# k and q of the last MoBA heads in seven block products instead of eight

## The chip, the cores and the metric

The kernel runs on one core of a Trainium2 chip. The metric is the device time of one launch in microseconds; the kernel before takes 423.49 us, the median of three runs from 423.46 to 423.8. Five engines work side by side and each takes its instructions in order: TensorE (PE in the profile; PEld is its weight load), VectorE (DVE), ScalarE (ACT), GpSimd (POOL) and SyncE (SP), which here only issues transfers. An instruction that waits holds up all that stand behind it on its engine or queue.

## The reference, cut to what matters

The input x has 512 tokens of 1024 values. One normalised copy h is multiplied by a wide matrix; its columns give q, k, v and z of eight forgetting heads and of eight MoBA heads, two gates, and the forget logits. Head dimension is 64, so half of the heads are 256 columns.

```python
h = rms_norm(x, norm_g)
proj = h @ w_in
fq, fk, fv, fz, mq, mk, mv, mz, ga, gb, fl = split_cols(proj, IN_SPLITS)
...
q = partial_rope(rms_norm(to_heads(mq, MOBA_HEADS), moba_q_g), positions)
k = partial_rope(rms_norm(to_heads(mk, MOBA_HEADS), moba_k_g), positions)
v = to_heads(mv, MOBA_HEADS)
y_moba = from_heads(moba_attention(q, k, v)) * jax.nn.silu(mz)
merged = sigmoid(ga + b_gate[0]) * (y_fox @ w_fox) + sigmoid(gb + b_gate[1]) * (y_moba @ w_moba)
x = x + merged @ w_out
```

With 512 tokens and blocks of 256, the MoBA attention is plain causal attention: there are two blocks, and each token may look at its own and the one before.

## The kernel before, in words

Every product is made of three passes: each float32 operand is split into a high and a low part (`split`, L131: ScalarE copies the high part, VectorE subtracts it from the raw one), and high x high, high x low and low x high are summed in a PSUM bank. The left side, the normalised input transposed, lies in SBUF as Gh and Gl, eight chunks of 128 rows by 512 tokens. Weights come in raw pieces of 128 x 4 x 256 (512 KB each) into the four buffers of tag wr; their parts lie in four buffers each of tags wh and wl.

The heads come in four groups: fox a, fox b, moba a, moba b. For each name (mkb is k of the second four MoBA heads, mqb their q) `unit` (L386) multiplies a tile of 128 tokens by the 256 columns, 24 matmuls, and `evac_qk` (L309) copies the bank out; after every second tile `norm_qk` (L321) squares, reduces, takes a power on GpSimd (L333, ff) and scales q or k by it on GpSimd (L335), and `do_rope` (L360) rotates the first 16 values of each head in four GpSimd instructions (L365 to L371).

`attn_group` (L512) is the attention of four heads. `Tr` transposes q and k of two heads into p_qT and p_kT (L522, L524), makes QS, KH and KL from them on ScalarE and VectorE, and copies KH to the other half of the partitions with a transfer. `Aa` makes the logits lg (L558, L559) and the exponentials, `Bb` transposes these (p_a, p_b, p_cc, L602), splits them and multiplies by v into pv (L612, L613). The banks of p_qT, p_kT, p_a, p_b and p_cc are three of tag tp in turn. The fox heads use four rows of KL beside k for the forget terms; `moba_begin` (L490) clears these rows on GpSimd before the MoBA heads use the tiles.

While a group's attention runs, the products of the next group are put between its parts (`plan`, L1218, and `inter`, L1178): while moba a is computed, mkb, mqb and half of mvb. `group_2` (L720) makes two names at once in seven block products instead of eight (Strassen's scheme in Winograd's form): left operands are four blocks A11, A12, A22 of the input and sums S1 to S4 of its blocks, right operands are blocks of raw weights and differences of them (`sub`, L728). In the kernel before only GZ0, z of the MoBA heads, is made so; the code for GQ0 (mkb and mqb) is there and not called. The sums S1 to S4 are computed by VectorE early (`make_sums`), stored to DRAM in two parts (s_dramh, s_draml) and fetched into slots: slot A is the tiles Q20, Q21 (once the fox heads have done with them) and two others; a second slot holds the next sum. S1 replaces the first sum in slot A when that has been read, S4 the second.

A scheduler sets the order on each engine, by its own estimate of when things are ready, so instructions of several parts interleave. Loads go through SP's queue in the scheduled order. rbc (L237) is a row used only before the attention.

Of the kernel before, what the change touches and what calls it, by code (L numbers as in the profile page):

```python
# [7 lines left out]
F32 = mybir.dt.float32  # L8
F32R = mybir.dt.float32r
AF = mybir.ActivationFunctionType  # L10
OP = mybir.AluOpType
AX = mybir.AxisListType

P = 128
S = 512
# [3 lines left out]
HD = 64  # L19
# [6 lines left out]
C_NG, C_BG, C_FQ, C_FK, C_MQ, C_MK, C_BF, C_GQ, C_GK, C_END = 0, 8, 24, 25, 26, 27, 28, 36, 52, 68  # L26
# [3 lines left out]
def fox_moba_kernel(ctx: ExitStack, tc, xT, x, w_in, w_fl, w_fox, w_moba, w_out, cst, rope, out):  # L30


    nc = tc.nc
    V, A, G, T = nc.vector, nc.scalar, nc.gpsimd, nc.tensor

    con = ctx.enter_context(tc.tile_pool(name="con", bufs=1))
    sb = ctx.enter_context(tc.tile_pool(name="sb", bufs=1))
# [198 lines left out]

    rbc = con.tile([P, S], F32, name="rbc")  # L237

# [82 lines left out]
    def norm_qk(name, ts):  # L321
# [10 lines left out]
        f2 = ff.rearrange("p t h -> p (t h)")  # L332
        G.tensor_tensor(out=f2, in0=ss.rearrange("p t h -> p (t h)"), in1=mh, op=OP.pow)  # L333
        q3 = qn.rearrange("p t (h d) -> p (t h) d", d=HD)
        G.tensor_tensor(out=q3, in0=q3, in1=f2[:, :, None].to_broadcast([P, 8, HD]), op=OP.mult)  # L335

# [153 lines left out]
    def moba_begin():  # L490
        for o in range(2):
            rows = slice(HD, HD + 32) if o == 0 else slice(0, 32)
            for tl in KLt[o]:
                G.memset(tl[rows, :].bitcast(F32), 0.0)

# [200 lines left out]
    Z_ORDER = (0, 1, 3, 5, 4, 2, 6)  # L696
    Q_ORDER = Z_ORDER

# [21 lines left out]
    def group_2(name):  # L720
        gq = name == "GQ0"
        first, second = ("mkb", "mqb") if gq else ("mza", "mzb")
        order_ = Q_ORDER if gq else Z_ORDER
        porder = order_
        st, R, B, slots = {}, {}, {}, {}
# [13 lines left out]
        def prep(n):  # L739
# [9 lines left out]
            return go  # L749
        for key in ("11", "12", "22", "21"):  # L750
            last = max(porder.index(n) for n in {"11": (0, 4), "12": (1, 3, 5), "21": (2, 5), "22": (6, 1, 3)}[key])
            loads.append((load(key), base + last))
# [266 lines left out]
    def group_o():  # L1019
# [94 lines left out]
        def evac(n):  # L1114
# [13 lines left out]
            else:  # L1128
# [7 lines left out]

    order = ["fqa", "fka", "fza", "fzb", "fva", "fkb", "fqb", "fvb", "mka", "mqa", "mva", "mkb", "mqb", "mvb", "GZ0", "wf0", "wf1", "wf2", "wf3",
             "GA0", "GA1", "GB0", "wm0", "wm2",
# [70 lines left out]
    for k, u in enumerate(fz):  # L1209
        u()  # L1210
        if k < 3:
# [7 lines left out]
            ("f", "b", C_FQ, C_FK, ["mka", "mqa", "mva"]),  # L1219
            ("m", "a", C_MQ, C_MK, ["mkb", "mqb", "mvb:01"]),  # L1220
            ("m", "b", C_MQ, C_MK, ["mvb:23", "GZ0", "wf0"]))
# [166 lines left out]
```

## Time and profile before

| | |
|---|---|
| median of three runs | 423.49 us (423.46 to 423.8) |
| the profiled execution | 423.75 us, its span 422.0 us |
| TensorE busy | 414.9 us (98%), 2956 matmuls |
| VectorE busy | 333.2 us (79%), 571 instructions |
| ScalarE busy | 273.6 us (65%) |
| GpSimd busy | 107.0 us (25%) |
| TensorE clock granted | 1.000 over the span, that is 2.4 GHz |

Busy time is what the profile shows between the start and the end of an engine's instructions, overlaps counted once. Matmuls are pipelined: one of 256 columns shows some 0.28 us, and the next starts before it ends, so the distance between starts is what it costs. The moba a attention with mkb, mqb and mvb stands at about 160 to 220 us, the moba b attention with GZ0 and the first of the output products (f, tiles pf) from there to 275 us, and the gate products (GA0 and on) behind that.

### The profile page before, as it was taken

What the parts mean: (1) busy time and instruction counts of PE and PEld (TensorE: products, weight loads), DVE (VectorE), ACT (ScalarE), POOL (GpSimd) and SP (SyncE); (2) the same over time, 40 slices, a digit from 0 to 9 for tenths busy, and PEclk for the clock granted to TensorE, in tenths of its full rate; (3) what the DMA queues carried; (4) which work ended last, traced back from release to release, by engine and by line L of the source; (5) the groups of instructions that cost most, each with busy time, mean ns of one, the idle gap of its engine ahead of it and who ended that gap; (6) DMA issues with size and microseconds to landing.
All of it is one profiled execution on the core that took longest, in us unless ns stands there. A gap on an engine that the chain in (4) does not pass through costs nothing.

```text
span 422.0 us, 7872 instructions
## 1 busy us (share of the span) xinstructions
PE 414.9 (98%) x2956; PEld 388.1 (92%) x2956; DVE 333.2 (79%) x571; ACT 273.6 (65%) x521; POOL 107.0 (25%) x127
## 2 busy tenths in 40 slices
PE   7999999999999999999999999999999999999996
PEld 6998899999999999999999998899999989988884
DVE  5669978797878997596977997637989675788982
ACT  4975437878769866796568876446847525685550
POOL 1049300252114690317600125120000020022240
PEclk9999999999999999999999999999999999999999
DMA  7981144654263662231048736623141726796394
GB/s 236 400 324 51 56 144 124 189 171 155 50 210 80 223 193 73 78 110 43 0 127 239 266 120 222 244 99 110 37 164 53 247 51 151 238 247 112 84 163 155
DMA packets 29703, 63.73 MB, mean 151 GB/s; under 512 B 3424, under 2 KB 10272, under 8 KB 29664
## 3 DMA queue, kind: packets, MB, share of 16 engines
q1 hardware_dynamic: 16880, 42.57, 30.3%
q0 software_dynamic: 3968, 9.44, 10.3%
q10 hardware_dynamic: 8816, 11.21, 9.1%
q8 instruction: 23, 0.38, 0.4%
q14 instruction: 16, 0.13, 0.1%
HBM read 52.56 MB, written 6.32 MB: 140 GB/s over the span
## 4 chain that ended last, share of the span: by engine, by line
PE 82%; DMA 6%; DVE 6%; ACT 2%; issue 1%; POOL 1%; SPq 1%; DVEq 0%; ACTq 0%
PE pb_GA L907 3%; PE pb_GB L907 3%; PE pb_GA L906 3%; PE pb_GB L904 3%; PE pb_GA L904 3%; PE pb_GB L906 3%; PE po L1093 3%; PE po L1091 3%; PE po L1092 3%; PE lg L559 2%; PE lg L558 2%; PE pv L613 2%; PE pv L612 2%; PE pGZ0a L771 2%; PE pGZ0b L771 2%; DMA x<-in_x_dram 2%
## 5 line engine op out<-in xcount | busy, mean ns | idle before, releaser
L333 POOL TENSOR_TENSOR ff<-ss,mh 128x8 f32<-128x8 f32 x16 | 27.8, 1741 | 60.6 <-DVE ss L331 51.8
L563 ACT ACTIVATE p<-p,negm 128x128 f32<-128x128 f32 (+1 forms) x64 | 35.7, 558 | 8.7 <-DVE negm L561 8.3
L561 DVE CUSTOM_DVE_ANT_0 p<-lg,mask 128x128 f32<-128x128 f32 (+1 forms) x64 | 30.2, 484 | 8.5 <-PE lg L559 8.2
L134 ACT ACTIVATE wh_GB<-wr_gb 128x1024 fp32r<-128x1024 f32 x14 | 14.6, 1058 | 13.4 <-PE pm L670 5.9
L136 DVE TENSOR_TENSOR wl_GA<-wr_ga,wh_GA 128x1024 fp32r<-128x1024 f32 x14 | 17.6, 1266 | 6.2 <-ACT wh_GA L134 6.2
L558 PE MATMUL lg<-KH,QS 128*128 128x128 f32 (+1 forms) x64 | 21.0, 333 | 0.2 <-DMA KH<-KH 0.2
L1053 ACT ACTIVATE wh_o<-wr_o 128x1024 fp32r<-128x1024 f32 x14 | 14.8, 1058 | 9.7 <-PE pb_GB L906 2.8
L974 POOL DMA_DIRECT2D uGB<-f x4 | 3.5, 869 | 69.4 <-issue 59.4
L136 DVE TENSOR_TENSOR wl_GB<-wr_gb,wh_GB 128x1024 fp32r<-128x1024 f32 x14 | 16.8, 1220 | 5.0 <-ACT wh_GB L134 5.0
L134 ACT ACTIVATE wh_GA<-wr_ga 128x1024 fp32r<-128x1024 f32 x14 | 14.6, 1059 | 9.2 <-PE pb_GA L906 5.9
L1054 DVE TENSOR_TENSOR wl_o<-wr_o,wh_o 128x1024 fp32r<-128x1024 f32 x14 | 16.9, 1218 | 2.4 <-ACT wh_o L1053 2.4
L532 DVE SCALAR_TENSOR_TENSOR QS<-p_qT,cs,QS 64x512 fp32r<-64x512 f32 x16 | 12.0, 750 | 4.1 <-ACT QS L531 3.7
L531 ACT ACTIVATE QS<-p_qT,cs 64x512 fp32r<-64x512 f32 x16 | 10.9, 680 | 4.1 <-PE p_qT L522 2.8
L904 PE MATMUL pb_GB<-Gh,wh_GB 128*128 128x256 f32 x48 | 13.5, 281 | 0.0
L904 PE MATMUL pb_GA<-Gh,wh_GA 128*128 128x256 f32 x48 | 13.5, 281 | 0.0
L906 PE MATMUL pb_GB<-Gl,wh_GB 128*128 128x256 f32 x48 | 13.5, 281 | 0.0
L906 PE MATMUL pb_GA<-Gl,wh_GA 128*128 128x256 f32 x48 | 13.5, 281 | 0.0
L907 PE MATMUL pb_GB<-Gh,wl_GB 128*128 128x256 f32 x48 | 13.5, 281 | 0.0
L907 PE MATMUL pb_GA<-Gh,wl_GA 128*128 128x256 f32 x48 | 13.5, 281 | 0.0
L669 PE MATMUL pf<-yhf,wh_wf 128*128 128x512 f32 x32 | 12.9, 402 | 0.0
L670 PE MATMUL pf<-ylf,wh_wf 128*128 128x512 f32 x32 | 12.7, 396 | 0.0
L558 PEld LDWEIGHTS lg<-KH,QS 128*128 128x128 f32 x64 | 12.1, 189 | 0.6 <-issue 0.3
(479 smaller groups left out, 1820.0 us busy)
## 6 DMA issues: line engine op xcount, KB each, us to landing
wr_ga<-in_w_in_dram SPq DMA_DIRECT2D x8, 512.0 KB
wr_gb<-in_w_in_dram SPq DMA_DIRECT2D x8, 512.0 KB
wr_o<-in_w_out_dram SPq DMA_DIRECT2D x8, 512.0 KB
xt<-in_xT_dram SPq DMA_DIRECT2D x8, 256.0 KB
x<-in_x_dram SPq DMA_DIRECT2D x8, 256.0 KB
KH<-KH ACTq DMA_DIRECT2D x16, 128.0 KB
s_dramh<-sum_h ACTq DMA_DIRECT2D x8, 256.0 KB
s_draml<-xt ACTq DMA_DIRECT2D x8, 256.0 KB
```

Source lines behind the costliest of these rows:

```text
L134: A.activation(hi[:, :, 0:n], src, AF.Copy)
L136: eng.tensor_tensor(out=lo[:, q, 0:n], in0=src[:, q], in1=hi[:, q, 0:n].bitcast(F32), op=OP.subtract)
L333: G.tensor_tensor(out=f2, in0=ss.rearrange("p t h -> p (t h)"), in1=mh, op=OP.pow)
L558: T.matmul(lg[:, :n], qs[:, qt], kh[:, :n], start=True, stop=False)
L561: V.tensor_tensor_reduce(pt, lg[:, :n], mask[:, 512 - n:512], -0.125, 3.0e38, op0=OP.add, op1=OP.min, accum_out=mkn[:, hh, i:i + 1])
L563: A.activation(pt, pt, AF.Exp, bias=mkn[:, hh, i:i + 1], scale=-1.0, accum_out=rs[:, hh, i:i + 1])
L771: T.matmul(o, x, y, start=(new and h == 0 and k == 0 and i == 0), stop=(k == 3 and i == 2), skip_group_check=True)
L904: T.matmul(o, hi[:, k, cc], lh, start=(n < 3 and c == 0 and k == 0), stop=False, skip_group_check=True)
L906: T.matmul(o, hi[:, k, cc], ll, start=False, stop=False, skip_group_check=True)
L907: T.matmul(o, lo[:, k, cc], lh, start=False, stop=(k == 3), skip_group_check=True)
L1053: A.activation(wide(hi), wide(R[key, c]), AF.Copy)
L1054: V.tensor_tensor(out=wide(lo), in0=wide(R[key, c]), in1=wide(hi).bitcast(F32), op=OP.subtract)
```

## The change

mkb and mqb are taken from the list of plain products and GQ0 stands in their place. Its order of products is A11, A12, S2, S3, S1, A22, S4 (indices 0, 2, 3, 1, 4, 5, 6), that of its weight splits 0, 2, 1, 3, 4, 5, 6, and the four raw weights are loaded as 11, 21, 12, 22. For these two names the scaling in `norm_qk` is on VectorE. The forget rows are cleared by four transfers, each copying four zero rows of the same tile over them, on SP's queue. rbc becomes a tile of tag row, whose buffer the second slot uses later.

```diff
@@ -234,7 +234,7 @@
         V.tensor_scalar(e2, mm, EPS, None, op0=OP.mult)
         G.tensor_tensor(out=r, in0=mm, in1=mh[:, :NT], op=OP.pow)
 
-    rbc = con.tile([P, S], F32, name="rbc")
+    rbc = sb.tile([P, S], F32, name="rbc", tag="row", bufs=1)
 
 
     def norm_row():
@@ -332,7 +332,7 @@
         f2 = ff.rearrange("p t h -> p (t h)")
         G.tensor_tensor(out=f2, in0=ss.rearrange("p t h -> p (t h)"), in1=mh, op=OP.pow)
         q3 = qn.rearrange("p t (h d) -> p (t h) d", d=HD)
-        G.tensor_tensor(out=q3, in0=q3, in1=f2[:, :, None].to_broadcast([P, 8, HD]), op=OP.mult)
+        (V if name in ("mqb", "mkb") else G).tensor_tensor(out=q3, in0=q3, in1=f2[:, :, None].to_broadcast([P, 8, HD]), op=OP.mult)
 
     def evac_v(p, name, t):
         if name not in VT:
@@ -490,8 +490,9 @@
     def moba_begin():
         for o in range(2):
             rows = slice(HD, HD + 32) if o == 0 else slice(0, 32)
+            a = rows.start
             for tl in KLt[o]:
-                G.memset(tl[rows, :].bitcast(F32), 0.0)
+                nc.sync.dma_start(out=tl[a:a + 4, :].bitcast(F32), in_=tl[a + 4:a + 8, :].bitcast(F32))
 
 
     Y = {}
@@ -694,7 +695,7 @@
     groups = {}
     SLOT = {}
     Z_ORDER = (0, 1, 3, 5, 4, 2, 6)
-    Q_ORDER = Z_ORDER
+    Q_ORDER = (0, 2, 3, 1, 4, 5, 6)
 
     def sums_slot(name, kind):
         if kind == "A":
@@ -721,7 +722,7 @@
         gq = name == "GQ0"
         first, second = ("mkb", "mqb") if gq else ("mza", "mzb")
         order_ = Q_ORDER if gq else Z_ORDER
-        porder = order_
+        porder = (0, 2, 1, 3, 4, 5, 6) if gq else order_
         st, R, B, slots = {}, {}, {}, {}
         base = len(preps)
 
@@ -747,7 +748,7 @@
                     sub("12", "21", "12")
                 B[n] = split(R[("11", "12", "21", "12", "11", "12", "22")[n]], CW, f"{name}{n}")
             return go
-        for key in ("11", "12", "22", "21"):
+        for key in ("11", "21", "12", "22") if gq else ("11", "12", "22", "21"):
             last = max(porder.index(n) for n in {"11": (0, 4), "12": (1, 3, 5), "21": (2, 5), "22": (6, 1, 3)}[key])
             loads.append((load(key), base + last))
         preps.extend(prep(n) for n in porder)
@@ -1134,7 +1135,7 @@
         groups["WO"] = late_loads
 
 
-    order = ["fqa", "fka", "fza", "fzb", "fva", "fkb", "fqb", "fvb", "mka", "mqa", "mva", "mkb", "mqb", "mvb", "GZ0", "wf0", "wf1", "wf2", "wf3",
+    order = ["fqa", "fka", "fza", "fzb", "fva", "fkb", "fqb", "fvb", "mka", "mqa", "mva", "GQ0", "mvb", "GZ0", "wf0", "wf1", "wf2", "wf3",
              "GA0", "GA1", "GB0", "wm0", "wm2",
              "GB1", "wm1", "wm3", "WO"]
     for nm in order[2:]:
@@ -1217,7 +1218,7 @@
     rope_tables()
     plan = (("f", "a", C_FQ, C_FK, ["fkb", "fqb", "fvb"]),
             ("f", "b", C_FQ, C_FK, ["mka", "mqa", "mva"]),
-            ("m", "a", C_MQ, C_MK, ["mkb", "mqb", "mvb:01"]),
+            ("m", "a", C_MQ, C_MK, ["GQ0", "mvb:01"]),
             ("m", "b", C_MQ, C_MK, ["mvb:23", "GZ0", "wf0"]))
     head, body, tail, gate = attn_group("f", "a", col(C_FQ), col(C_FK))
     head[0]()
```

VectorE, in the stretch where the last products before mkb end and the attention of moba a begins. Names: mqb0 is the upper half of mqb's raw weights, GQ03 the split for product 3 (S2), wr_mkb0 and wr_mqb1 are raw weights that differences overwrite. Before:

```order
L609 TENSOR_TENSOR ptl_2291<-p_a_2280,pth_2290 128x512
L343 TENSOR_TENSOR v_mva_2221<-pj_mva2_2328,v_mva_2221 128x4x64
L532 SCALAR_TENSOR_TENSOR QS_2238<-p_qT_2228,cs_66,QS_2238 64x512
L536 SCALAR_TENSOR_TENSOR KL00_855<-p_kT_2229,cs_66,KH_2239 64x512
L609 TENSOR_TENSOR ptl_2295<-p_b_2285,pth_2294 128x512
L532 SCALAR_TENSOR_TENSOR QS_2245<-p_qT_2228,cs_66,QS_2245 64x512
L136 TENSOR_TENSOR wl_mqb0_2447<-wr_mqb0_1940,wh_mqb0_2446 128x4x256
L536 SCALAR_TENSOR_TENSOR KL10_856<-p_kT_2229,cs_66,KH_2246 64x512
L343 TENSOR_TENSOR v_mva_2221<-pj_mva3_2395,v_mva_2221 128x4x64
L136 TENSOR_TENSOR wl_mqb1_2551<-wr_mqb1_2077,wh_mqb1_2550 128x4x256
L609 TENSOR_TENSOR ptl_2302<-p_cc_2298,pth_2301 128x256
```

Now, from the same row on (p_a has another number there):

```order
L610 TENSOR_TENSOR ptl_2289<-p_a_2278,pth_2288 128x512
L510 TENSOR_TENSOR ylf2_2118<-ypair_1927,yhf2_2117 128x512
L343 TENSOR_TENSOR v_mva_2219<-pj_mva2_2324,v_mva_2219 128x4x64
L610 TENSOR_TENSOR ptl_2293<-p_b_2283,pth_2292 128x512
L136 TENSOR_TENSOR wl_GQ01_2445<-wr_mqb0_1940,wh_GQ01_2444 128x4x256
L343 TENSOR_TENSOR v_mva_2219<-pj_mva3_2391,v_mva_2219 128x4x64
L730 TENSOR_TENSOR wr_mqb0_1940<-wr_mqb1_2077,wr_mkb0_1677 128x1024
L533 SCALAR_TENSOR_TENSOR QS_2236<-p_qT_2226,cs_66,QS_2236 64x512
L537 SCALAR_TENSOR_TENSOR KL00_855<-p_kT_2227,cs_66,KH_2237 64x512
L610 TENSOR_TENSOR ptl_2300<-p_cc_2296,pth_2299 128x256
L136 TENSOR_TENSOR wl_GQ03_2450<-wr_mqb0_1940,wh_GQ03_2449 128x4x256
L533 SCALAR_TENSOR_TENSOR QS_2243<-p_qT_2226,cs_66,QS_2243 64x512
```

Where two splits stood among the attention's work, two splits and a difference stand now ahead of the second QS, and a further difference and split come right behind these rows.

SP's queue, at the loads for the same part. mvb0, mvb1, mza0 and mzb0 are raw weights; Q20, Q21 and the tiles GQ0_a (or GZ0_a) are slot A, slot_b the second slot. Before:

```order
L210 DMA wr_mqb0_1940<-in_w_in_dram 128x1024
L210 DMA wr_mqb1_2077<-in_w_in_dram 128x1024
L712 DMA Q20_853<-s_dramh_128 128x512
L712 DMA GZ0_a0_3210<-s_draml_129 128x512
L712 DMA GZ0_a1_3211<-s_draml_129 128x512
L210 DMA wr_mvb0_2194<-in_w_in_dram 128x1024
L210 DMA wr_mvb1_2326<-in_w_in_dram 128x1024
L712 DMA Q21_854<-s_dramh_128 128x512
L736 DMA wr_mza0_2450<-in_w_in_dram 128x1024
L736 DMA wr_mzb0_2554<-in_w_in_dram 128x1024
```

Now, from the weights of mvb on; the first four loads of sums here are S1, the next four S4:

```order
L210 DMA wr_mvb0_2504<-in_w_in_dram 128x1024
L210 DMA wr_mvb1_2576<-in_w_in_dram 128x1024
L713 DMA Q20_853<-s_dramh_128 128x512
L713 DMA GQ0_a0_2453<-s_draml_129 128x512
L713 DMA Q21_854<-s_dramh_128 128x512
L713 DMA GQ0_a1_2454<-s_draml_129 128x512
L737 DMA wr_mza0_2578<-in_w_in_dram 128x1024
L713 DMA slot_b3_2459<-s_dramh_128 128x512
L713 DMA slot_b1_2461<-s_draml_129 128x512
L713 DMA slot_b0_2460<-s_dramh_128 128x512
L713 DMA slot_b2_2462<-s_draml_129 128x512
L737 DMA wr_mzb0_2680<-in_w_in_dram 128x1024
```

Before, GZ0's first sum was fetched here, long before GZ0. Now the first sums of GQ0 stand ahead of these rows, S1 and S4 behind the weights of mvb, and those of GZ0 come later.

## Rows read from the trace of the kernel before

**Rows 1.** page, part 1: engine, busy us (share of the span), instructions
```profile
PE 414.9 (98%) x2956; PEld 388.1 (92%) x2956; DVE 333.2 (79%) x571; ACT 273.6 (65%) x521; POOL 107.0 (25%) x127
```

**Rows 2.** waits of TensorE, 140 to 262 us: us in total, times, longest
```profile
PE p_qT L522 <- POOL qn_mqa L371: 0.3, 1, 0.3
PE lg L558 <- DMA KH<-KH: 0.2, 1, 0.2
```

**Rows 3.** timeline of TensorE, 183 to 194 us: start us, us, engine, line
```profile
183.24 0.28 PE L306 MATMUL pj_mqb<-wl_mqb,Gh 128*128 128x256 f32 x1
...
185.83 0.28 PE L307 MATMUL pj_mqb<-wh_mqb,Gl 128*128 128x256 f32 x1
...
193.23 0.60 PE L602 MATMUL p_a<-ident,p 128*128 128x128 f32 x4
193.67 0.60 PE L602 MATMUL p_b<-ident,p 128*128 128x128 f32 x4
```

**Rows 4.** windows: us; busy PE, PEld, DVE, ACT, POOL (instructions); clock; DMA share; GB/s
```profile
160.00:220.00 60.00, 59.83 (x488) 58.66 (x487) 46.84 (x90) 42.46 (x92) 21.86 (x26) 1.00 0.25 76
220.00:260.00 40.00, 39.99 (x285) 37.25 (x283) 35.54 (x73) 33.52 (x72) 9.16 (x10) 1.00 0.59 189
140.00:260.00 120.00, 119.47 (x927) 115.05 (x926) 100.25 (x198) 90.01 (x196) 48.33 (x57) 1.00 0.42 131
```

**Rows 5.** lines of VectorE, 140 to 262 us: busy us, mean ns, idle before
```profile
L327 DVE TENSOR_REDUCE ss<-sq 128x8 f32<-128x512 f32 x6 | 4.0, 672 | 0.0
...
L136 DVE TENSOR_TENSOR wl_mqb<-wr_mqb,wh_mqb 128x1024 fp32r<-128x1024 f32 x2 | 2.4, 1220 | 0.1
...
L651 DVE TENSOR_TENSOR ypair<-ypair,rinv_bc 128x512 f32<-128x512 f32 x2 | 1.4, 689 | 0.0
...
L792 DVE TENSOR_TENSOR uGZ<-pGZ0b,uGZ 128x512 f32<-128x512 f32 x2 | 1.4, 677 | 0.0
...
L729 DVE TENSOR_TENSOR wr_mza<-wr_mzb,wr_mza 128x1024 f32<-128x1024 f32 x1 | 1.2, 1225 | 0.0
```

**Rows 6.** timeline of TensorE, the last matmuls of f
```profile
274.20 0.39 PE L669 MATMUL pf<-yhf,wh_wf 128*128 128x512 f32 x1
...
276.52 0.40 PE L670 MATMUL pf<-ylf,wh_wf 128*128 128x512 f32 x1
```

**Rows 7.** lines of ScalarE, 140 to 262 us
```profile
L134 ACT ACTIVATE wh_mqb<-wr_mqb 128x1024 fp32r<-128x1024 f32 x2 | 2.1, 1060 | 0.0
...
L312 ACT ACTIVATE qn_mqb<-pj_mqb 128x256 f32<-128x256 f32 x4 | 1.5, 377 | 1.1 <-PE pj_mqb L307 1.0
...
L788 ACT ACTIVATE uGZ<-pGZ0a 128x512 f32<-128x512 f32 x2 | 1.2, 593 | 1.3 <-PE pGZ0a L771 1.3
```

**Rows 8.** lines of GpSimd, 140 to 262 us
```profile
L333 POOL TENSOR_TENSOR ff<-ss,mh 128x8 f32<-128x8 f32 x7 | 11.6, 1660 | 20.1 <-DVE ss L331 11.7 <-ACT qn_mqa L312 8.3
...
L335 POOL TENSOR_TENSOR qn_mqb<-qn_mqb,ff 128x512 f32<-128x512 f32 x2 | 2.5, 1226 | 0.1
...
L365 POOL TENSOR_TENSOR ra<-qn_mqb,tab_mq 128x128 f32<-128x128 f32 x2 | 1.8, 893 | 0.2
```

**Rows 9.** timeline of GpSimd, 140 to 150 us
```profile
144.42 0.52 POOL L494 MEMSET KL<- 32x512 f32 x1
...
147.60 1.30 POOL L650 TENSOR_TENSOR rinv_bc<-zs_fzb,rinv_bc 128x512 f32<-128x512 f32 x1
```

**Rows 10.** timeline of VectorE, 140 to 160 us
```profile
147.61 2.38 DVE L136 TENSOR_TENSOR wl_mkb<-wr_mkb,wh_mkb 128x1024 fp32r<-128x1024 f32 x1 [0.50 <-ACT wh_mkb L134]
...
150.47 1.93 DVE L136 TENSOR_TENSOR wl_mkb<-wr_mkb,wh_mkb 128x1024 fp32r<-128x1024 f32 x1
```

**Rows 11.** timeline of SP's queue, 150 to 260 us
```profile
226.69 0.33 SPq L712 DMA_DIRECT2D Q<-s_dramh  x1
```

**Rows 12.** readers of tile Q: ns min/median/max, first and last start us
```profile
L771 PE MATMUL pGZ0a<-Q,wh_GZ x8: 276/282/287, 234.0 to 236.8; 128*128 128x256 f32 x8
```

**Rows 13.** DMA issues: count, KB each, median us from issue to landing
```profile
uGB<-f POOLq DMA_DIRECT2D x4, 256.0 KB, 3.3
```

## The prediction

> **What bounds the kernel now.** The busy rows of the page come first: TensorE is busy for 414.9 of 422.0 us, VectorE for 333.2, ScalarE for 273.6, GpSimd for 107.0 [rows 1]. A busy TensorE may still be waiting in part, so the waits come next: between 140 and 262 us, where the last heads are computed, all that TensorE waited for by name is 0.3 us for a rotation on GpSimd, at 153 us, and 0.2 us for a transfer [rows 2]. The timeline says at what pitch it works: in the product of mqb, 22 starts of 256-column matmuls lie between 183.24 and 185.83 us, 0.118 us each [rows 3]. The reader is to see an unbroken stream: every matmul removed there is worth its pitch, as long as nothing else becomes late. So the question is what the change asks of the engines that feed the stream, and the windows answer how much room they have: from 160 to 220 us VectorE is busy for 46.84 of 60 us, from 220 to 260 us (where GZ0 already runs in seven products) for 35.54 of 40 us, TensorE being busy for 39.99 of those 40; over 140 to 260 us VectorE has 100.25 of 120 us and ScalarE 90.01 [rows 4].
>
> **The change, part by part.**
>
> *Matmuls.* Before, mkb and mqb take 2 names x 4 token tiles x 24 = 192 matmuls of 256 columns. After, 7 products x 2 halves x 4 chunks x 3 = 168 of the same shape. 24 x 0.118 = 2.83 us go from TensorE, all of it on the path, since the engine has no gaps to lose them in. The transposes and the attention matmuls keep their number.
>
> *VectorE gets fourteen instructions.* Four differences of raw weights, 128x1024: 4 x 1.225 = 4.90 us. Seven splits in place of four: 3 x 1.22 = 3.66 us. Three sums of a bank and a kept block, 128x512: 3 x 0.68 = 2.04 us. Four scalings that GpSimd did, for which the nearest row is the 128x512 multiplication of ypair at 0.689: 2.76 us. Together 13.4 us [rows 5]; nothing is taken from it. From 160 to 220 us it has 60 - 46.84 = 13.2 us idle, so within that stretch it would be full. What gives it room is the order: 12 matmuls of f (pitch 0.232 us, [rows 6]) and 24 of GA0 that stood behind the last pv matmul stand ahead of it now, 2.8 + 2.8 = 5.6 us of TensorE work beside the same VectorE work. The stretch of 140 to 260 us becomes 120 - 2.83 + 5.6 = 122.8 us long for 100.25 + 13.4 = 113.6 us of VectorE, 92.5%. What that costs has no row, so two ends. At the lower end nothing: 88.9% (35.54 of 40) went with no wait of TensorE over 0.2 us [rows 2, 4], and no row shows a limit there. At the upper end 88.9% is the most that this engine can do without holding the others: then 113.6 us need 127.8, and TensorE waits 5.0 us. I add the durations along the new order from the transposes of p_a before product A11 on. VectorE then comes at the next ones 0 to 2 us late; where it is late, the first to feel it is a transpose (p_cc, p_b) that needs a bank of tag tp which VectorE still reads through its KL and QS rows, by about 0.4 us once, perhaps twice. The value taken is 0.7 us, near the lower end, as the row with the densest VectorE speaks for it.
>
> *The chain that ends in the transposes of mqb.* After product S4: copy 0.59, square about the same, reduction 0.67, power 1.66, scaling 0.69, the first step of the rotation 0.9 and three shorter ones, put at 0.4 each: 6.3 us [rows 5, 7, 8]. Between it and the transposes the new order has 126 matmuls of 256 columns, 14.9 us. VectorE's own queue takes some of the cover, since the last scaling stands behind two splits and differences of GZ0; by the durations along the order some 3 us are left. Cost nothing; if that cover goes, TensorE stands before p_qT as it does at 153 us, and the excess is paid one for one.
>
> *ScalarE.* Three more splits, four copies of 128x512 for eight of 128x256: 3 x 1.06 + 4 x 0.593 - 8 x 0.377 = +2.5 us [rows 7], 92.5 of 122.8 us. Hidden.
>
> *GpSimd and the forget rows.* It loses four scalings of about 1.2 and four clearings of 0.52 us [rows 8, 9]. The clearing at 144.42 stands in the run of GpSimd work that ends in the rotation TensorE waits for at 153 us, so 0.3 us could be had there [rows 2, 9]; but a product of zs and rinv, waiting for a transfer, stands in the same run, so I take 0 between -0.3 and 0. The four transfers in their place move 8 KB each on SP's queue. Those of KL_857 and KL_858 wait there for the last fox logits that read them, and sums for product S2 are queued behind; from the later of those logits to that product there are 129 matmuls of 256 columns, 15.2 us, twice what such a load needs (below). Cost 0; it would be the part above 15 us otherwise. The move of rbc to another pool issues nothing.
>
> *Transfers of sums.* Sixteen more of 256 KB, 4.2 MB. 160 to 220 us moved 76 GB/s [rows 4], 4.6 MB; 8.8 MB in 57 us is 154 GB/s, under the 189 of 220 to 260 us. The place that is tight is the second load of the slot of S2: S1 may be fetched only when product S2 has been read, and product S1 begins after product S3 alone, some 25 matmuls of 256 columns and 19 others: 25 x 0.118, 12 of 128 columns at 0.11, 4 of 512 at 0.232 and 3 between, put at 0.18: 5.7 us [rows 3, 6]. For how long such a load takes there are bounds: 3.3 us from issue to landing for 256 KB on GpSimd's queue, and at most 7.3 us from the first issue at 226.69 to the first reader at 234.0 us, where nobody waited [rows 2, 11 to 13]. So TensorE waits 0 to 1.6 us; the first two of the four pieces are enough to begin, so I take 0. Queued ahead of them on SP are the two weights of mvb, which wait for VectorE; these are the first to make it worse.
>
> *Sum.* On the profiled execution's 423.75 us: -2.83 + 0.7 = 421.6 us. It lay 0.26 us above the median of the runs, 423.49; so 421.4 us.
>
> **VectorE beside GpSimd.** The split of mkb at 147.61 took 2.38 us and the next 1.93, where the same instruction takes 1.22 elsewhere; beside the first GpSimd was multiplying and rotating [rows 5, 9, 10].
> The Trainium skill, "SBUF — State Buffer", section "Who interferes with whom", says that a VectorE instruction with two SBUF inputs and a GpSimd instruction that reads SBUF shut each other out for a whole instruction; the trace agrees, with 2.38 for 1.22 us, and the rule speaks against this change, since eleven of the fourteen new instructions have two SBUF inputs.
> By the rows alone: each of the eleven could lose up to 1.16 us, 12.8 in all, if GpSimd were always at work. It is busy for 21.86 of 60 us [rows 4] and its four scalings of some 4.5 us go, which leaves 30%: about 3 us more of VectorE, 95% of the stretch.
>
> **The rivals.**
> 1. *VectorE becomes the bound, slower.* Place: products S2 to S4, where the new order has nearly as much VectorE as TensorE work. For it: 13.4 us into 13.2 us of room, and 92.5% where 88.9% is the most shown. Against it: the stretch is stretched by 5.6 us of other matmuls, and VectorE's idle time before was waiting for ScalarE and TensorE, not need. Decides once VectorE holds TensorE for more than 2.83 + 0.85 us. Price 5.0: 423.49 - 2.83 + 5.0 = 425.7, with 424.4 to 428.
> 2. *GpSimd holds VectorE, slower.* The loss at its full 12.8 us gives 126.4 us of VectorE in 122.8: at least 3.6 us of waiting, 424.3 and up. Against it: GpSimd is idle two thirds of the time and loses work.
> 3. *The load of S1 takes the gain, no change.* A wait of 1.6 us at product S1, as much again at product S4 or behind the weights of mvb, on top of 0.7 us: 423.49 - 2.83 + 0.7 + 1.6 to 2.6 = 423.0 to 424.0. For it: 5.7 us of cover against up to 7.3. Against it: the two first pieces suffice and the same kind of load was waited for by nobody in GZ0.
> 4. *More than forecast.* No wait of TensorE and the 0.3 us before p_qT gone as well: 420.4.
>
> **How the numbers follow.** Forecast 0.57, with its own range 420.8 to 422.4; rival 1 0.13, rival 2 0.06, rival 3 0.19, rival 4 0.05. A measurement of this kernel tells 0.2% (0.85 us) from no change: below 422.64 is faster, above 424.34 slower. Faster: 0.57 + 0.05 = 0.62; same 0.19; slower 0.13 + 0.06 = 0.19. The range 420.3 to 425.0 leaves out about half of rivals 1 and 2 above and a little below.
>
> **What would show it.** In the changed kernel's profile: 24 fewer matmuls than the 2956 of before, give or take what is not recorded, at the old pitch of 0.118; VectorE busy for about 347 us; no TensorE wait over 0.5 us by name between 140 and 265 us. Starts of matmuls that lie apart at products S1 or S3 with a transfer as the releaser would prove rival 3; waits of p_cc, p_b, lg or a product for a VectorE row, rival 1; splits and differences of GQ0 at 1.9 us and more, all through, rival 2. The forecast is wrong if the stream of matmuls from mva to GZ0 has gaps that add up to more than 2 us, or if the time is outside 420.8 to 422.4 without any.

## The result, and the profile after

The changed kernel takes 426.63 us (median of 5 runs, 426.05 to 429.42) where the kernel before, on the same chip, takes 423.8 (423.46 to 424.33): a ratio of 1.0078, 95% interval 1.0055 to 1.0102. It is slower by about 3.3 us by the ratio; 421.4 had been forecast, with a range of 420.3 to 425.0. The profiled execution took 428.38 us with a span of 426.2, 4.2 longer than the span before. It lies 1.75 us above the median of its five, whose granted clocks run from 0.992 to 1.000 (0.996 here), so what the clock costs below is not in all of them.

Part 1 of the page after, beside [rows 1]:

```profile
PE 415.3 (97%) x2932; PEld 387.4 (91%) x2932; DVE 342.5 (80%) x585; ACT 275.5 (65%) x520; POOL 106.9 (25%) x119
```

The 24 matmuls are gone (2956 to 2932), but TensorE is busy for as long as before in a longer span. Adding up by how much the starts of matmuls lie further apart than is usual for their shape (its median distance in the kernel before) gives 16.0 us over the whole trace before and 22.4 after: 6.4 more waiting less 2.83 of matmuls is 3.6 us, most of the difference of the spans. Between 140 and 262 us alone it is 6.4 before and 12.4 after. So the work did get shorter; waiting more than took its place. The waits of TensorE by name, whole span (us in total, times, longest):

```profile
PE lg L559 <- DMA KH<-KH: 3.9, 3, 1.6
PE warm_ps L107 <- DVE fg_pre L466: 1.5, 1, 1.5
PE pGQ0a L772 <- DMA Q<-s_dramh: 0.7, 1, 0.7
```

The second stands at the start of the kernel before too. The other two are new, and both are transfers: beside [rows 2], 0.2 us for KH's copy has become 3.9. Neither of the new ones is for VectorE. The windows, first of the kernel after, beside [rows 4]:

```profile
160.00:220.00 60.00, 57.75 (x466) 56.25 (x465) 52.96 (x99) 43.19 (x88) 21.17 (x27) 1.00 0.46 144
220.00:260.00 40.00, 37.53 (x252) 34.14 (x251) 30.85 (x57) 28.81 (x59) 5.12 (x3) 0.96 0.57 181
180.00:200.00 20.00, 17.75 (x138) 16.79 (x137) 17.06 (x35) 14.39 (x31) 4.61 (x7) 1.00 0.75 243
200.00:220.00 20.00, 20.00 (x167) 19.82 (x166) 18.88 (x37) 13.30 (x29) 14.64 (x16) 1.00 0.24 74
246.00:250.00 4.00, 4.00 (x13) 3.24 (x13) 3.84 (x8) 3.18 (x7) 0.51 (x1) 0.57 0.46 119
```

Two things are to be read here. From 200 to 220 us VectorE is busy for 18.88 of 20 us, 94%, and TensorE for all 20: a full VectorE does not hold it. From 180 to 200 us the DMA engines are busy for 0.75 of the time, 243 GB/s, and there TensorE loses 2.25 us. The same 20 us of the kernel before:

```profile
180.00:200.00 20.00, 20.00 (x164) 19.66 (x164) 15.38 (x35) 16.29 (x37) 9.71 (x16) 1.00 0.26 81
```

What moved into that stretch is told by SP's queue. Before, the first sums of GZ0 (tiles Q and GZ_a) were fetched early, into slots that nobody used:

```profile
141.94 0.33 SPq L712 DMA_DIRECT2D Q<-s_dramh  x1
146.48 2.15 SPq L712 DMA_DIRECT2D GZ_a<-s_draml  x2
...
152.81 0.42 SPq L712 DMA_DIRECT2D Q<-s_dramh  x1
```

After, GQ0 uses that slot for S2 and then S1, so the same loads of GZ0 come once S1 has been read, right behind S1, S4 and the weights of GZ0:

```profile
175.00 0.38 SPq L713 DMA_DIRECT2D Q<-s_dramh  x1
...
179.13 0.32 SPq L713 DMA_DIRECT2D slot_b<-s_dramh  x1
...
182.72 0.97 SPq L737 DMA_DIRECT2D wr_mzb<-in_w_in_dram  x2
186.46 1.03 SPq L713 DMA_DIRECT2D Q<-s_dramh  x2
187.55 0.90 SPq L713 DMA_DIRECT2D GZ_a<-s_draml  x2
```

And the chain of waits after (start, us, what) has the four transfers for which TensorE, directly or through ScalarE, stood:

```profile
175.00 7.50 DMA Q<-s_dramh
...
186.18 5.54 DMA KH<-KH
...
223.22 7.59 DMA wr_wf<-in_w_fox_dram
...
242.46 3.13 DMA KH<-KH
```

S1's third piece took 7.50 us where 5.7 us of cover had been counted. (Cover is the time from a transfer's issue to the moment at which the engine has nothing else left to do before it needs the data.) The copy of KH, 128 KB, issued on ScalarE's queue at 186.18, took 5.54 us beside SP's loads. Three copies are waited for:

```profile
191.76 0.33 PE L559 MATMUL lg<-KH,QS 128*128 128x128 f32 x1 [1.43 <-DMA KH<-KH]
...
232.23 0.30 PE L559 MATMUL lg<-KH,QS 128*128 128x128 f32 x1 [0.84 <-DMA KH<-KH]
...
245.63 0.33 PE L559 MATMUL lg<-KH,QS 128*128 128x128 f32 x1 [1.63 <-DMA KH<-KH]
```

Slow copies are not new, though. In the kernel before, the copy issued at 233.30 us took 6.41 us (issue to landing by the trace's semaphores), and the logit that reads it started without a gap, since it had 6.5 us of cover:

```profile
233.30 0.48 ACTq L535 DMA_DIRECT2D KH<-KH  x1
...
239.82 0.27 PE L558 MATMUL lg<-KH,QS 128*128 128x128 f32 x1
```

So each copy has to be held against its cover. These are the copies that were waited for, and those in like places elsewhere, from the traces of both kernels and of four runs told below (us):

| kernel | copy issued at: took, cover | | |
|---|---|---|---|
| before | 181.01: 3.48, 4.9 | 214.66: 4.17, 4.0 | 233.30: 6.41, 6.5 |
| after | 186.18: 5.54, 4.0 | 223.91: 8.18, 7.3 | 242.46: 3.13, 1.3 |
| run 1 | 186.48: 3.40, 4.2 | 224.07: 7.55, 7.7 | 243.32: 2.95, 1.4 |
| run 3 | 189.32: 5.99, 7.5 | 222.04: 6.53, 8.4 | 239.31: 2.34, 3.5 |
| run 6 | 184.83: 6.46, 4.0 | 223.44: 8.64, 7.3 | 241.36: 2.45, 2.3 |
| run 8 | 212.63: 5.92, 3.9 | 234.45: 7.12, 3.9 | |

The last wait of the changed kernel is not that of a slow copy: the copy was issued only 1.3 us before TensorE had nothing else to do, and the quickest copies in these traces took 2.2 us. That issue is late by ScalarE's order, which the third row of the chain leads into:

```profile
230.90 1.06 ACT L134 ACTIVATE wh_wf<-wr_wf 128x1024 fp32r<-128x1024 f32 x1 [3.63 <-DMA wr_wf<-in_w_fox_dram]
```

ScalarE stands for 3.63 us before the first split of wf0, whose weights were queued behind GZ0's second loads; QS, KH and the exponentials that stand behind it come late. Right after the wait that ended at 245.63 us the granted clock of 246 to 250 us is 0.57, and eight matmuls of f (512 columns) go at the lower level, 1.2 GHz:

```profile
246.25 0.63 PE L670 MATMUL pf<-yhf,wh_wf 128*128 128x512 f32 x1
246.67 0.63 PE L671 MATMUL pf<-ylf,wh_wf 128*128 128x512 f32 x1
```

Their pitch is 0.43 us where it was 0.232 [rows 6]: from 246.25 to the start of the ninth at 249.60 us it is 3.35 us for 8 x 0.232 = 1.86, 1.5 us more for having waited. The waits by name and the clock, 3.9 + 0.7 + 1.5 = 6.1 us, are as much as the starts between 140 and 262 us have moved apart.

The Trainium skill, "DMA: Bandwidth & Descriptors", section "Issuing engines are not separate DMA queues", says that transfers started by ScalarE, SyncE or GpSimd run on the same 16 DMA engines and interleave. The trace agrees: a copy on ScalarE's own queue takes 5.54 us beside SP's loads, and 3.40 at the same place in run 1, without the sixteen loads of sums. The prediction asked only when SP's queue would serve the sums, not what they would meet.

### The profile page after: what moved, and what is told of

Same layout as the page of the kernel before. It is cut to its first block, busy times and chain, and to the rows that moved or that the text cites. A ratio compares the mean times of both kernels' runs of the same rounds, so it can differ in the third digit from the quotient of the medians.

```text
span 426.2 us, 7861 instructions
## 1 busy us (share of the span) xinstructions
PE 415.3 (97%) x2932; PEld 387.4 (91%) x2932; DVE 342.5 (80%) x585; ACT 275.5 (65%) x520; POOL 106.9 (25%) x119
## 4 chain that ended last, share of the span: by engine, by line
PE 77%; DMA 9%; POOL 4%; issue 4%; ACT 3%; SPq 1%; DVE 1%; ACTq 0%; DVEq 0%; POOLq 0%
PE pb_GA L908 3%; PE pb_GB L908 3%; PE pb_GA L907 3%; PE pb_GA L905 3%; PE pb_GB L905 3%; PE pb_GB L907 3%; PE po L1093 3%; PE po L1094 3%; PE po L1092 3%; PE pGQ0a L772 2%; DMA KH<-KH 2%; PE pf L670 2%; PE pf L671 2%; PE pf L672 2%; DMA wr_wf<-in_w_fox_dram 2%
## 5 line engine op out<-in xcount | busy, mean ns | idle before, releaser
L333 POOL TENSOR_TENSOR ff<-ss,mh 128x8 f32<-128x8 f32 x16 | 29.0, 1821 | 62.0 <-DVE ss L331 61.5
L638 ACT ACTIVATE ysh<-pv 64x512 f32<-64x512 f32 x16 | 9.5, 593 | 6.8 <-PE pv L614 4.0
```

## The experiments

The theories named in the expectations. **T**: the transfers of sums, the new ones and those moved, make KH's copies, S1's pieces and wf's weights late. **V**: VectorE is too full between 140 and 260 us. **Q**: the clearing of the forget rows on SP's queue, and the order that follows from it, holds the work. **R** (formed after run 8): what the matmuls give is lost or kept by where the order happens to put KH's copies among the large loads; any edit that lays the order anew may lose it. The runs were measured in four sets, each with its own measure of the kernel before beside it (us, medians); the ratio of the changed kernel itself is 1.0078 (1.0055 to 1.0102). A profile is of one execution and shows its waits, not the median's: in runs 1, 4, 7, 8, 9 and 11 it was the longest of its run (427.31, 428.75, 426.45, 433.40, 427.84, 424.99 us).

| run | kernel | time | before | 95% interval of the ratio |
|---|---|---|---|---|
| 1 | after, no loads of sums for q, k | 424.08 | 423.64 | 0.9988 to 1.0020 |
| 2 | before, with those 16 loads, unread | 424.69 | 423.64 | 0.9999 to 1.0042 |
| 3 | after, forget rows cleared on GpSimd | 423.45 | 423.64 | 0.9977 to 1.0011 |
| 4 | after, scaling on GpSimd | 427.91 | 423.64 | 1.0068 to 1.0108 |
| 5 | after, KH's second half by ScalarE | 423.81 | 423.74 | 0.9983 to 1.0018 |
| 6 | after, wf0, wf1 loaded by GpSimd's queue | 426.61 | 423.74 | 1.0045 to 1.0106 |
| 7 | 3 and 5 together | 424.97 | 423.74 | 1.0019 to 1.0050 |
| 8 | before, less 24 matmuls | 429.39 | 423.74 | 1.0115 to 1.0185 |
| 9 | before, KH by ScalarE | 425.52 | 423.83 | 1.0024 to 1.0069 |
| 10 | 8 and KH by ScalarE | 420.45 | 423.83 | 0.9898 to 0.9946 |
| 11 | 5, with mqa's scaling on VectorE | 422.82 | 423.83 | 0.9958 to 0.9994 |
| 12 | before, forget rows cleared on SP | 423.48 | 423.83 | 0.9969 to 1.0011 |
| 13 | 11, with A22 ahead of S1 | 426.55 | 423.81 | 1.0039 to 1.0088 |
| 14 | 13, with mqb's rotation on VectorE | 425.76 | 423.81 | 1.0029 to 1.0068 |
| 15 | 5, no loads of sums for q, k | 422.49 | 423.81 | 0.9959 to 0.9993 |

**Run 1.** The products S1 to S4 of GQ0 read a quarter of Gh and Gl, and nothing is fetched for them.

```diff
-                    lh, ll = left_2(what, k)
+                    lh, ll = left("A21", k) if gq and what[0] == "S" else left_2(what, k)
...
-                if n == order_[0]:
+                if n == order_[0] and not gq:
...
-                if n in sums[:2]:
+                if n in sums[:2] and not gq:
```

> The changed kernel, but GQ0 multiplies blocks of the input that already lie in SBUF in place of the sums S1 to S4, and fetches no sums (q and k of the last heads are wrong for that): same matmuls, VectorE, ScalarE and GpSimd work, 4.2 MB of transfers less. Theory T (the new transfers delay the copies of KH, the sums themselves and the weights of f, and TensorE waits for these): the waits go, the 24 matmuls are won: 420.5 to 421.8 us against 423.8 of before. Theory V (VectorE has too much to do between 140 and 260 us): no change against the changed kernel, 426 to 427 us. Theory Q (the order of SP's queue and the clearing transfers): within 1 us of the changed kernel.

424.08: some 2.5 us below the changed kernel, between what T and the other two had. The waits at 181 and 190 us are gone and GZ0's first sums are fetched at 144 to 154 again; others remain or have come:

```profile
PE p_qT L523 <- POOL qn_mqa L371: 1.5, 1, 1.5
PE pv L613 <- ACT pth L609: 1.5, 1, 1.5
PE lg L559 <- DMA KH<-KH: 1.3, 1, 1.3
```

The table above tells the three copies apart. The first has nearly the cover that it has in the changed kernel (4.2 us for 4.0) and takes 3.40 us for 5.54, so its wait of 1.4 us is the price of the loads. The third is issued as late as there and waited for without any of the loads, and ScalarE stands before wf's split for 3.50 us here too; so neither is their doing. The loads are a large part, not all.

**Run 2.** The kernel before, with the sixteen loads, which nothing reads; rbc gives up its own place, as in the change.

```diff
-    rbc = con.tile([P, S], F32, name="rbc")
+    rbc = sb.tile([P, S], F32, name="rbc", tag="row", bufs=1)
...
+                        if at == 0:
+                            slots[0], slots[1] = sums_slot("GQ0", "A"), sums_slot("GQ0", "B")
+                            sums_load(slots[0], "S2")
+                            sums_load(slots[1], "S3")
+                        elif at == 3:
+                            sums_load(slots[0], "S1")
+                        else:
+                            sums_load(slots[1], "S4")
```

> The kernel before with eight products per pair as it was, and the sixteen transfers of sums added at the places where the changed kernel has them, read by nobody (rbc in the tag row, as in the changed kernel, since the slot needs it). Theory T: the transfers alone cost what the changed kernel lost, some 4 to 7 us if their timing is met, at least 2: 425.5 to 430 us. Theory V: nothing, 423 to 424.5 us.

424.69, an interval that just touches no change: the traffic alone costs some 1 us, less than the 2 us at the least that T had. TensorE waits 1.3 us before a logit at 188.61 us; the profile names a ScalarE instruction, and KH's copy there, 4.39 us for 3.1 us of cover, had landed only 0.14 us earlier.

**Run 3.** The memsets of the forget rows stand on GpSimd again.

```diff
-            a = rows.start
             for tl in KLt[o]:
-                nc.sync.dma_start(out=tl[a:a + 4, :].bitcast(F32), in_=tl[a + 4:a + 8, :].bitcast(F32))
+                G.memset(tl[rows, :].bitcast(F32), 0.0)
```

> The changed kernel with the forget rows cleared on GpSimd again. Theory T and theory V: within 0.8 us of the changed kernel's 426.6, since four transfers of 8 KB are neither traffic nor VectorE work. Theory Q (these transfers hold SP's queue until the fox heads have read their rows, so that the loads behind them start late and together): 1.5 to 3 us faster, 423.5 to 425 us.

423.45, 3 us below the changed kernel; TensorE's waits between 140 and 260 us:

```profile
PE p_qT L522 <- POOL qn_mqa L371: 1.0, 1, 1.0
...
PE pGQ0a L771 <- DMA Q<-s_dramh: 0.6, 1, 0.6
```

No logit waits for a copy in this order, though the DMA engines are busier still (281 GB/s at 180 to 200 us) and two copies take 5.99 and 6.53 us: they have 7.5 and 8.4 us of cover. It looked like Q, but the loads that stand behind the clearing on SP's queue, the first and the last piece of S2, are issued at 142.76 and 153.65 us here and at 142.66 and 153.38 in the changed kernel: the clearing did not hold them. Run 12 agrees.

**Run 4.** `(V if name in ("mqb", "mkb") else G).tensor_tensor` is `G.tensor_tensor` again.

> The changed kernel with the four scalings of mkb and mqb on GpSimd again: 2.8 us less for VectorE. Theory V: 1 to 3 us faster than the changed kernel, 423.6 to 425.6 us. Theory T: no gain from it, 426 to 427.5 us.

427.91: with less work on VectorE it is no faster (GpSimd has that work instead), and lg waits 2.4 us for KH's copies. V falls, with the full VectorE at 200 to 220 us shown above.

**Run 5.** In the MoBA heads the copy is gone; it becomes a second ScalarE instruction.

```diff
-                    nc.scalar.dma_start(out=kh[ot, :].bitcast(F32), in_=kh[me, :].bitcast(F32))
+                    if fox:
+                        nc.scalar.dma_start(out=kh[ot, :].bitcast(F32), in_=kh[me, :].bitcast(F32))
+                    else:
+                        A.activation(kh[ot, :], pk[me, :], AF.Copy, scale=gk[me, :])
```

> The changed kernel, with the second half of KH of the last heads (mqb, mkb and mqa, mka) written by ScalarE straight from the transposes' bank, with gk as scale (8 more ScalarE instructions of about 0.68 us), where a transfer through the queue of ScalarE copied it. Theory T (the products' sums now travel in bursts, and the small copies, S1's pieces and wf's weights come late beside them): the logits' waits for KH at 190 (1.59 us), 231 (1.17) and 243 (1.87) go or become waits for ScalarE of under 0.5 us each; the stop of ScalarE at wf's split (3.63 us before 230.9) stays, as its load is not touched. Time 424 to 425 (before 423.6, after 426.6). Theory Q (the order that follows from clearing on SP's queue holds the work, the copies only show it): the same gaps come back in front of other instructions, and the time stays within 0.5 us of 426.6.

423.81, just below the 424 to 425 that T had. All waits of TensorE above 0.4 us after the start:

```profile
PE p_qT L523 <- POOL qn_mqa L371: 1.5, 1, 1.5
PE p_qT L523 <- POOL qn_mqb L371: 0.8, 1, 0.8
PE pGQ0a L775 <- DMA Q<-s_dramh: 0.5, 1, 0.5
```

The 3.9 us before lg are gone, 2.3 us for GpSimd have come. The order is another one: ScalarE's stop at wf's split, which T had staying, is 1.1 us for 3.63.

**Run 6.** One word, and the only run in which ScalarE's instructions stand in exactly the order of the changed kernel.

```diff
-                nc.sync.dma_start(out=raw[0], in_=w[n, :, 4 * hf:4 * hf + 4, :])
+                (nc.gpsimd if name in ("wf0", "wf1") else nc.sync).dma_start(out=raw[0], in_=w[n, :, 4 * hf:4 * hf + 4, :])
```

> The changed kernel, with the two loads of wf0's and the two of wf1's weights put on GpSimd's queue (wf0's alone move in the order) instead of SP's, where they stood behind the second loads of GZ0's sums; ScalarE's order is word for word that of the changed kernel. Theory T, its third part (ScalarE stands at wf0's first split because the weights are queued behind the sums, and QS, KH and the exponentials behind it come late): the load is issued 1 to 3 us earlier, ScalarE's stop of 3.63 us at 230.9 falls below 1.5 us, the logits' waits at 231 and 243 (1.17 and 1.87 us) and the stretch at half clock after 246 go with it, the wait at 190 (1.59) stays. Time 423.5 to 424.8. If the 16 DMA engines are simply full there (0.80 of 220 to 240 us), an earlier place in a queue moves the delay to the sums of GZ0 instead: a wait of TensorE for Gh or Q of 1 to 3 us at 225 to 235, and the time stays at 426 to 427.

426.61, nothing won. The loads were issued 1.0 us earlier, ScalarE stood for 2.28 instead of 3.63 us, and in the profiled execution, the shortest of six, there is no wait at 243; but the other two waits for KH are longer, 2.4 us the longest. With TensorE's and ScalarE's order held, the covers of the first two copies are the same, 4.0 and 7.3 us; the third has 2.3 us for 1.3. Its chain has these transfers:

```profile
184.83 6.46 DMA KH<-KH
...
222.19 6.80 DMA wr_wf<-in_w_fox_dram
...
241.36 2.45 DMA KH<-KH
```

The third part of T isn't borne out as a cause of its own: the execution that was profiled won, the median did not. What the rows give is the price of a copy: 2.45 us where the DMA engines are busy for 0.35 of the time (240 to 260 us), 6.46 beside the loads.

**Run 7.** The edits of runs 3 and 5.

> The changed kernel with both the forget rows cleared on GpSimd again (as in the run with that edit alone, 423.45 us) and the second half of KH of the MoBA heads written by ScalarE. Theory T: what that run had left (p_qT 1.0 us at 154, pGQ0a 0.6 at 181, and smaller ones) is mostly not KH; the time is 422.5 to 423.5, and the matmuls' 2.8 us is regained only in part. Theory Q: 423.2 to 423.7, as with the clearing alone.

424.97, above both theories: p_qT waits 2.0 us for qn_mqa, and 1.2 us go before a pv. Two edits that each gain 3 us do not add up; here run 5's edit costs 1.5.

**Run 8.** The matmuls by themselves.

```diff
-                T.matmul(p[:, :n], Gh[:, kk, st], lo[:, k, :n], start=False, stop=False)
+                if name not in ("mkb", "mqb") or kk not in (1, 3, 5):
+                    T.matmul(p[:, :n], Gh[:, kk, st], lo[:, k, :n], start=False, stop=False)
```

> The kernel before, leaving out 24 matmuls of 256 columns of mkb and mqb (three of the high by low products in each of the 8 units), so that q and k of the last heads miss a small part: the worth of the matmuls that the change removes, without its sums, its splits, its transfers or its order. If TensorE is the bound there, 24 x 0.118 = 2.83 us go: 420.6 to 421.2. If something else holds these stretches as soon as TensorE gets shorter (VectorE, the transfers), less than 1.5 us goes: 422.2 or more, and the change had nothing to win in the first place.

429.39: less work, no new load, no new instruction, and 5.7 us slower. Neither end of the expectation holds. The waits and the chain:

```profile
PE lg L559 <- DMA KH<-KH: 5.0, 2, 3.1
PE pb_GB L905 <- ACT wh_GB L134: 1.9, 1, 1.9
```

```profile
212.63 5.92 DMA KH<-KH
...
234.45 7.12 DMA KH<-KH
```

The copy at 212.63 stands right behind four loads of Gh and Gl (210.53 to 212.04 us), the one at 234.45 behind eight loads from 227.85 on. These are GZ0's own loads, which the kernel before has as well, and there too a copy among them took 6.41 us; but it had 6.5 us of cover, and these two have 3.9 each for 5.92 and 7.12. The order was laid anew, and the cover went with it; the granted clock, 0.987 in the profiled execution, adds its part. Theory R comes from here.

**Run 9.** Run 5's edit in the kernel before.

> The kernel before, with the second half of KH of the last eight heads written by ScalarE from the transposes' bank instead of by a transfer, as in the run that did the same to the changed kernel (423.81 us against 426.6). Theory T (the gain of that run came from taking the copies away from the bursts): in the kernel before no logit waits for a copy, so nothing is won: 423.2 to 424.3. If the edit is worth something by itself wherever it stands: below 422.0, and the run on the changed kernel says nothing of the change.

425.52, above what T had: where copies cost 0.2 us in all, the edit loses 1.7 us (TensorE waits 1.4 us before p_a at 251 to 253 us and 1.6 for a split of GB). So the edit has no worth of its own, and run 5's gain fits the copies' going; that the new order of run 5 had a part in it is not excluded.

**Run 10.** Run 8 with run 5's edit.

> The kernel before less 24 matmuls (mkb and mqb miss a small part, as in the run of 429.39 us) and with KH's second half written by ScalarE. In that run the logits waited twice for KH's copy (5.0 us, 3.1 us the longest) though it loads no sums for q and k at all. Theory R (a tuned order: the copies of KH had 4 to 5 us of cover by their place between GZ0's loads, and any edit that lays the order anew may lose it; the matmuls themselves are worth their 2.83 us): without copies the gain comes out, 420.6 to 421.8. Theory T in its strict form (only the new loads of sums make the copies late) has no account of the 429.39 and would have this run at 428 or more.

420.45, 3.3 us below the kernel before by the ratio (2.3 to 4.3): without copies the matmuls' worth of 2.83 comes out. The window:

```profile
140.00:260.00 120.00, 120.00 (x928) 115.79 (x927) 102.27 (x198) 95.40 (x205) 49.55 (x58) 1.00 0.39 128
```

TensorE is busy for all of the 120 us. Between runs 8 and 10 lie one edit, which takes the copies away and has the order laid anew, and 8.9 us.

**Run 11.** Run 5, and `("mqa", "mqb", "mkb")` for the names that VectorE scales.

> The changed kernel with KH's second half written by ScalarE (423.81 us alone) and mqa's scaling on VectorE too, like that of mqb and mkb. What the run with KH alone had left: p_qT waits for GpSimd's qn_mqa 1.5 us at 154, for qn_mqb 0.8, and S1's pieces 0.8. With two scalings of 1.05 to 1.5 us fewer on GpSimd before 154 the first wait goes: 422.0 to 423.0. If VectorE is what is full there (18.1 of 20 us), the wait comes back as one for VectorE and the time is 423.5 to 424.5.

422.82, below the kernel before and 3.8 below the changed one: the wait of 1.5 us for qn_mqa is gone, as expected (0.9 us for VectorE's v_mva has come). It is the fastest kernel here that computes all of the reference, by 0.24% (0.06 to 0.42).

**Run 12.** The edit undone in run 3, done alone in the kernel before.

> The kernel before with only the forget rows cleared by transfers on SP's queue (the edit of the change that carries no arithmetic). Theory Q (clearing on SP holds the loads queued behind it, and the order that follows is worse): 425 to 427. Theory R (its effect in the changed kernel, 3 us, came from the order that it happened to give, and is no price of a transfer): within 423.0 to 425.0, and where it is slower the waits stand at KH's copies, not at 142 to 154 where the transfers are. Theory T: 423.6, no effect.

423.48, no effect; TensorE waits for nothing by name between 140 and 260 us. The transfers that clear the rows cost nothing here, and in the changed kernel the loads behind them come no later than in run 3. So Q falls as a price of the clearing, and run 3's 3 us are put down to the order that came with it, as R has it.

**Runs 13 to 15** ask what is left between runs 5 and 10, 3.4 us. Run 13 has `Q_ORDER = (0, 2, 3, 1, 5, 4, 6)`, with the splits in that order; run 14 besides does the four instructions of `do_rope` on VectorE for mqb.

> The run that beat the kernel before (KH's second half by ScalarE, mqa's scaling on VectorE, 422.82 us) with one thing more: the product A22 stands ahead of S1 (order 0, 2, 3, 1, 5, 4, 6, its splits in that order too), so the reload of S1 has one more product, 2.8 us, before it is read. If what that run still lacks against 420.45 us is S1's late pieces (TensorE 19.47 of 20 us at 180 to 200) and the queue of GpSimd before the transposes of mqb (0.8 us at 217), the first goes and the second shrinks: 421.5 to 422.5. If the order laid anew costs elsewhere, as in most runs so far: 422.5 to 424.5.

> The same with the rotation of mqb on VectorE too (4 instructions of 128 x 64 to 128 x 128 for each half, some 1.0 us a half by the nearest rows) instead of GpSimd, where they took 0.3 to 1.4 us each at 211 to 217. If GpSimd's queue is what holds p_qT at 217: the wait of 0.8 us goes, 421.0 to 422.0. If VectorE, busy 19.3 of 20 us at 200 to 220, holds it, the wait gets longer: 423 or more.

426.55 and 425.76, both misses. In run 13 a piece of S1 is waited for still (0.9 us), and mqb's transposes for more:

```profile
PE p_qT L523 <- POOL qn_mqb L371: 2.5, 1, 2.5
```

In run 14 that wait is gone, and there are seven small ones of 0.2 to 0.9 us. Run 15 is run 5 without the loads, by run 1's edit (again q and k of the last heads are not the reference's):

> The changed kernel with KH's second half written by ScalarE (423.81 us) and without the sixteen loads of sums for q and k: the products S1 to S4 of GQ0 read a quarter of Gh and Gl in their place, so q and k of the last heads are wrong. What the loads still cost once no small copy travels beside them: theory T says S1's late pieces, 0.5 to 0.8 us, 423.0 to 423.3. If the loads cost nothing more and VectorE with GpSimd (p_qT's waits of 1.5 and 0.8 us) hold the rest, 423.6 to 424.0; if the loads were the whole loss, 420.5 to 421.5.

422.49: with no copy beside them, the sixteen loads are worth some 1.3 us by the medians, more than the 0.5 to 0.8 that T had. The last 2.0 us down to 420.45 were not taken apart: they hold the fourteen VectorE instructions and the chains over GpSimd, each with an order of its own.

## Why the prediction was wrong, step by step

*Matmuls*: right. 24 went, and run 10 gets their 2.83 us (3.3, interval 2.3 to 4.3) where nothing is late.

*VectorE*, 0.7 us: the fear was in the wrong place. It was busy for 342.5 us where 347 had been forecast, stood at 94% beside an unbroken TensorE, and no new wait of the changed kernel names it. Rivals 1 and 2 had times on the right side of before, and rival 1's range even holds the measured one, but by luck, for their reasons are not there: no transpose or logit waits for VectorE, and GQ0's splits took 1.21 and 1.31 us on average, not 1.9. (By its own share of 30%, the 12.8 us that GpSimd might cost VectorE come to 3.8 us, not to about 3; the forecast doesn't use it.)

*The chain to the transposes of mqb*: held here, no wait; but the 3 us of cover were thin, as 0.8 us in run 5 and 2.5 in run 13 show.

*ScalarE*, "hidden": it was free by its sum, yet it stood for 3.63 us for wf's weights; a sum of busy time does not see that. It makes the last copy's issue late, but run 1 has the stop and the late issue without the loads of sums, and run 6 couldn't make it a cause of its own.

*GpSimd and the forget rows*, 0: right for the clearing itself, by run 12 and by the times of the loads in run 3.

*Transfers of sums*, taken 0: this is the step that failed, in three ways. It averaged ("154 GB/s, under the 189"), where the loads come in bursts: 243 GB/s at 180 to 200 us. It looked for the tight place at S1 alone; there the wait was 0.7 us, inside the 0 to 1.6 given. And it never named two things that the new loads meet: GZ0's first sums, which had been fetched at 142 to 153 us into the slot that GQ0 now uses, and the copies of KH on another queue, whose cover was thin already (4.17 us for 4.0, and 6.41 for 6.5, in the kernel before). What the loads cost by name is 0.7 us at S1 and 1.4 at the first of KH's copies, 2.1 us where the sum has 0. Rival 3 did name S1, with 1.6 us and more for it; the copies are in none of the rivals.

*The frame* failed too: "every matmul removed there is worth its pitch, as long as nothing else becomes late" was taken as a default. Run 8 removed them and nothing else, and lost 5.7 us. What became late in the changed kernel besides the loads' 2.1 us is this: the other two of KH's copies, 0.8 and 1.6 us, and the slower clock behind the last, 1.5 us in the profiled execution. The last was late by its issue, 1.3 us before it was needed; the second took 8.18 us for 7.3 of cover, and whether the loads or the order made that difference (7.55 for 7.7 in run 1) is open.

Settled is which transfers TensorE stood for in the profiled execution, and that it is these and not VectorE. Not settled is how much of the 3 us is the sums' traffic (1.0 to 2.5 us by runs 1, 2 and 15) and how much the order that every edit laid anew: only run 6 held the order, and it moved no byte, only its time.

## What to carry to other kernels

Where a change adds transfers, list every small copy that the bound engine waits for within a few microseconds, on whatever queue, with its cover, and ask what each costs at the moment of the burst; a mean bandwidth does not tell it. A slow copy that is covered costs nothing (6.41 us here), and a quick one that is issued late does (3.13 us). Ask as well which loads had come early because a buffer stood idle, and when they come once it is used. And where a scheduler lays the order anew at each edit, measure the saving by itself before the change is built: here leaving 24 matmuls out moved the time by +5.7 us and, with KH's copies gone, by -3.3.

## What was not expected of the hardware

The same copy of 128 KB took 2.45 us in a quiet stretch and 5.5 to 8.2 beside loads of other queues. After the wait of 1.6 us that ended at 245.63 us TensorE's clock stood at its lower level for some 3.4 us (0.57 of full over 246 to 250 us), which nearly doubled the pitch of the matmuls that followed; after the wait of 1.4 us that ended at 191.76 us it did not fall (1.00 over 180 to 200 us).
